# The keys' first weight pieces: split in front of block 2's transposes, or one at a time behind block 3's

## The chip, the core and the metric

The kernel runs on one core of a Trainium2 chip. The core's engines take their instructions each from a queue of its own and wait for one another through semaphores: TensorE (PE in the profile, with its weight loads listed as PEld) does matrix products and transposes into PSUM; VectorE (DVE) and ScalarE (ACT) work element by element and read PSUM; GpSimd (POOL) does some elementwise work; SyncE (SP) issues nearly all DMA transfers. The metric is the device time of one execution in microseconds (us), lower is better.

## The reference

A two-layer decoder over 512 positions of width 1024. The first layer has a dilated windowed attention, the second a "forgetting" attention on keys and values that are projected once from the residual stream behind the first layer. Each layer ends in a gated feed-forward block with a short causal convolution. Cut to the place of the change:

```python
kvf  = rms_norm(h, kv_norm) @ w_kvf          # h is the residual stream after layer 0
k_sh = kvf[..., :B_WIDTH]                    # keys, 16 heads of 64
v_sh = kvf[..., B_WIDTH:2 * B_WIDTH]         # values
log_f = log_sigmoid(kvf[..., 2 * B_WIDTH:] + b_f)
c_sh = cumsum(log_f, axis=1)                 # bias of the forgetting attention
mix  = fox_mixer(rms_norm(h, g[0]), w_q_b, w_o_b, k_sh, v_sh, c_sh)
```

## The kernel before, in words

The 512 positions are four blocks (0 to 3) of 128. Every large product is made from three: both operands are split into a rounded high part and the low rest, and `mm3` (L229 to L231) adds high x high, high x low and low x high.

**Weights.** All weights come in pieces of 128 x 1024 numbers, in one fixed list. The class `Weights` carries each piece through three steps: `load` issues its DMA on SP into a raw buffer (L41), `high` casts it on ACT (L49) and `low` subtracts on DVE (L55); the pair is then ready for TensorE. `split(n)` runs the last two steps for all pieces below number n, and calls `load` for two pieces more. `get()` hands out the next pair and first splits as far as `ahead` tells: `self.split(self.n_get + self.ahead - 1)`, where `n_get` counts the pieces handed out. There are nine raw buffers (shared with other tiles of that size), and a load waits until its buffer is free.

**Order.** The program is written out by hand: each engine runs its instructions in the order in which the Python code issues them. Nothing is reordered by a scheduler. Buffers are taken from pools, and the semaphores that make a tile's user wait for its last readers come from that.

**Behind the first feed-forward block.** Its down-projection finishes the residual stream h block by block. For each block the class `SharedBoundary` has two steps. `norm(b)` takes the statistics on ACT and scales the block on DVE (xn, L413). `transpose(b)` transposes it on TensorE in eight pieces (L424, into two PSUM banks xt_ps); DVE multiplies by a gain (xf, L426); ACT rounds that to the high part (xkh, L431), DVE subtracts the low part (xkl, L432), and ACT keeps an ungained copy for the queries (nT, L434). xkh, xkl and nT come in two halves of 512 features each.

**First half of the values.** Blocks 0 and 1 are transposed while the down-projection still runs. Then block 3 is normed, and the values' first 512 columns are computed. Four weight pieces (512 x 512 by two of the eight feature groups each) are used over six steps: blocks 0 and 1 with pieces 0 and 1, then blocks 0 and 1 with pieces 2 and 3, then block 2 with 0 and 1, block 2 with 2 and 3, and the same for block 3. Block 2 is transposed in the middle of the second step, block 3 behind the third. The sums lie in four PSUM banks (v_ps), from which DVE (blocks 0 and 2) and ACT (blocks 1 and 3) copy them to Vt (L908).

**Behind it.** The keys follow in eight groups of 128 columns (k_ps, `keys(c)`), each with one weight piece; then the gates' bias (f_ps, behind the second key group), the second half of the values, the queries and the attention (scores s_ps).

When the first value product is reached, pieces 0 to 3 of this part (the values' weights) are already split. `ahead` is 4 there. So the second, third and fourth `get` each split one more piece, which is the weight of the key groups 0, 1 and 2.

Of the kernel before, what the change touches and what calls it, by code (L numbers as in the profile page):

```python
# [70 lines left out]
def trunk_kernel(ctx, tc, x, norm_gains, w_qkv_a, w_o_a, w_q_b, w_o_b, kv_norm, w_kvf, b_f,  # L71
# [11 lines left out]
    def t8(shape, dt=F32, name="t8"):  # L83
        return p8.tile(shape, dt, tag="t8", name=name)
# [7 lines left out]
    def bank(shape, name="bank"):  # L92
        return psp.tile(shape, F32, tag="ps", name=name)
# [68 lines left out]
    W = Weights(nc, new_raw, lambda: t8([128, 2, 1024], F32R, name="w"), pieces)  # L162
# [732 lines left out]
    def values(banks, w, s, blocks):  # L895
        for b in blocks:
            for k in range(2):
                kc = 2 * s + k
                ah, al = xs(bd2.xT, kc, slice(b * 128, b * 128 + 128))
                mm3(banks[b], ah, al, w[0][:, k, :], w[1][:, k, :], kc == 0, kc == KD - 1)  # L900

    def value_weight():
        return [t.rearrange("p (k c) -> p k c", k=2) for t in W.get()]

    def keep_values(hf, b, o):
        if b == 0:
            Vt[hf] = t8([128, 4, 512], name=f"Vt{hf}")
        (act.copy if b % 2 else dve.tensor_copy)(Vt[hf][:, b, :], o)  # L908

    bd2.norm(3)  # L910
    banks = [bank([128, 512], name="v_ps") for _ in range(4)]
    wv = []
    for sp_, blocks in ((0, (0, 1)), (2, (0, 1)), (0, (2,)), (2, (2,)), (0, (3,)), (2, (3,))):
        if len(wv) < 4:
            wv += [value_weight(), value_weight()]
        for b in blocks:
            for s in (sp_, sp_ + 1):
                values(banks, wv[s], s, (b,))
            if (sp_, b) == (2, 0):
                bd2.transpose(2)  # L920
                W.ahead = 3
        if (sp_, blocks) == (0, (2,)):
            bd2.transpose(3)
        if sp_ == 2 and blocks[-1] > 1:
            for bb in (blocks[0] - 2, blocks[0]):
                keep_values(0, bb, banks[bb])
# [305 lines left out]
```

## Time and profile before

| | |
|---|---|
| median of 3 runs | 1169.48 us (1168.93 to 1169.65) |
| profiled execution | 1168.88 us, its span 1167.1 us |
| TensorE busy | 1153.6 us of the span |
| VectorE, ScalarE, GpSimd busy | 663.8, 515.8, 203.9 us |
| DMA | 115.72 MB, 99 GB/s on average |

Times in the profile's lists are microseconds from the start of the span. A timeline row has the start, the length, the engine, the line of the source, the operation, "result <- inputs", and the number of instructions merged into the row; in brackets, where it is given, stands how long the engine had been idle before the row and who ended that wait. Lengths of neighbouring TensorE rows overlap, since products are pipelined: what a product costs is the distance to the next start. The chain of waits goes back from the last instruction and names at each step what released it.

### The profile page before, as it was taken

To read this page: it belongs to the slowest core of one execution; us is meant where nothing else is said; L and a number is where in the kernel's file an instruction comes from. 1 tells how busy PE (TensorE), PEld (TensorE's weight loads), DVE (VectorE), ACT (ScalarE), POOL (GpSimd) and SP (SyncE) were. 2 spreads that over 40 slices of the span, in tenths; PEclk is the share of its full clock that TensorE was granted. 3 is DMA by queue.
4 is the path that set the end of the run, shared out by engine and by line. 5 is a ranking of instruction groups with operands and counts; after the bars stand their busy time and mean duration, and the time that the engine had idled before them with its cause. 6 is when DMAs were issued, how large, how long until landed. Compare 5 with 4: busy or idle time off the path is not lost.

```text
span 1167.1 us, 15131 instructions
## 1 busy us (share of the span) xinstructions
PE 1153.6 (99%) x5898; PEld 960.1 (82%) x5898; DVE 663.8 (57%) x991; ACT 515.8 (44%) x900; POOL 203.9 (17%) x231
## 2 busy tenths in 40 slices
PE   9999999999999999999999999999999999999997
PEld 6888889888888888888778888789888888888886
DVE  6433586655655674406464788757566566575304
ACT  5444665333433463306462677755433334354202
POOL 2722000212212210000000565400122122120000
PEclk9999999999999999999999999999999999999999
DMA  8131063333333355203204344264332332244001
GB/s 294 53 110 37 3 182 109 103 97 108 90 91 108 93 167 169 60 1 85 81 1 128 100 119 126 76 201 126 91 109 83 99 108 88 93 145 162 1 1 72
DMA packets 134849, 115.72 MB, mean 99 GB/s; under 512 B 5753, under 2 KB 119913, under 8 KB 134778
## 3 DMA queue, kind: packets, MB, share of 16 engines
q1 hardware_dynamic: 133498, 110.57, 31.0%
q0 software_dynamic: 1280, 4.20, 1.5%
q8 instruction: 46, 0.75, 0.3%
q14 instruction: 25, 0.20, 0.1%
HBM read 108.41 MB, written 2.15 MB: 95 GB/s over the span
## 4 chain that ended last, share of the span: by engine, by line
PE 89%; DVE 5%; ACT 3%; issue 2%; DVEq 0%; ACTq 0%
PE up L231 12%; PE up L229 12%; PE up L230 12%; PE acc L229 9%; PE acc L230 9%; PE acc L231 9%; PE v_ps L229 2%; PE v_ps L231 2%; PE v_ps L230 2%; PE qk_ps L230 2%; PE qk_ps L229 2%; PE qk_ps L231 2%; PE first L229 1%; PE first L230 1%; PE first L231 1%
## 5 line engine op out<-in xcount | busy, mean ns | idle before, releaser
L55 DVE TENSOR_TENSOR w<-wraw,w 128x1024 fp32r<-128x1024 f32 x182 | 262.3, 1467 | 93.5 <-ACT w L49 93.0
L49 ACT CAST w<-wraw 128x1024 fp32r<-128x1024 f32 x182 | 184.9, 1048 | 61.6 <-PE acc L231 38.3
L517 ACT ACTIVATE bb<-up,conv 128x512 f32<-128x512 f32 x80 | 62.4, 780 | 272.8 <-PE up L231 272.8
L525 POOL TENSOR_TENSOR hT<-bb 128x512 f32<-128x512 f32 x44 | 92.8, 2108 | 490.8 <-DVE bb L520 348.9
L518 DVE SCALAR_TENSOR_TENSOR bb<-up,conv,bb 128x511 f32<-128x511 f32 x80 | 60.0, 749 | 173.0 <-ACT bb L517 173.0
L229 PE MATMUL acc<-w,hs 128*128 128x512 f32 (+1 forms) x356 | 138.0, 388 | 1.1 <-DVE mix L276 1.1
L230 PE MATMUL acc<-w,hs 128*128 128x512 f32 (+1 forms) x356 | 137.8, 387 | 0.0
L231 PE MATMUL acc<-w,hs 128*128 128x512 f32 (+1 forms) x356 | 137.8, 387 | 0.0
L229 PE MATMUL up<-xbh,w 128*128 128x512 f32 x320 | 124.6, 389 | 0.0
L230 PE MATMUL up<-xcl,w 128*128 128x512 f32 x320 | 124.6, 389 | 0.0
L231 PE MATMUL up<-xbh,w 128*128 128x512 f32 x320 | 124.6, 389 | 0.0
L230 PE MATMUL up<-xbl,w 128*128 128x512 f32 x320 | 124.6, 389 | 0.0
L229 PE MATMUL up<-xch,w 128*128 128x512 f32 x320 | 124.6, 389 | 0.0
L231 PE MATMUL up<-xch,w 128*128 128x512 f32 x320 | 124.6, 389 | 0.0
L229 PEld LDWEIGHTS acc<-w,hs 128*128 128x128 f32 x356 | 66.9, 188 | 14.9 <-DVE mix L276 1.3
L231 PEld LDWEIGHTS acc<-w,hs 128*128 128x128 f32 x356 | 66.9, 188 | 13.5
L230 PEld LDWEIGHTS acc<-w,hs 128*128 128x128 f32 x356 | 66.9, 188 | 13.5
L231 PEld LDWEIGHTS up<-xch,w 128*128 128x128 f32 x320 | 60.1, 188 | 12.6
L229 PEld LDWEIGHTS up<-xbh,w 128*128 128x128 f32 x320 | 60.1, 188 | 12.5
L230 PEld LDWEIGHTS up<-xbl,w 128*128 128x128 f32 x320 | 60.1, 188 | 12.5
L230 PEld LDWEIGHTS up<-xcl,w 128*128 128x128 f32 x320 | 60.1, 188 | 12.5
L231 PEld LDWEIGHTS up<-xbh,w 128*128 128x128 f32 x320 | 60.1, 188 | 12.3
(241 smaller groups left out, 2085.7 us busy)
## 6 DMA issues: line engine op xcount, KB each, us to landing
wraw<-in_w_up_dram SPq DMA_DIRECT2D x88, 512.0 KB
wraw<-in_w_down_dram SPq DMA_DIRECT2D x44, 512.0 KB
wraw<-in_w_kvf_dram SPq DMA_DIRECT2D x16, 512.0 KB
wraw<-in_w_qkv_a_dram SPq DMA_DIRECT2D x16, 256.0 KB
wraw<-in_w_q_b_dram SPq DMA_DIRECT2D x8, 512.0 KB
ck<-cd SPq DMA_DIRECT2D x8, 512.0 KB
qst<-qst POOLq DMA_DIRECT2D x16, 256.0 KB, 3.5
wraw<-in_w_o_b_dram SPq DMA_DIRECT2D x8, 512.0 KB
```

What stands on the lines that cost most here:

```text
L49: self.nc.scalar.copy(pair[:, 0], raw)
L55: self.nc.vector.tensor_tensor(pair[:, 1], raw, pair[:, 0].bitcast(F32), ALU.subtract)
L229: pe.matmul(o, ah, bh, start=first, stop=False, skip_group_check=shared)
L230: pe.matmul(o, ah, bl, start=False, stop=False, skip_group_check=shared)
L231: pe.matmul(o, al, bh, start=False, stop=last, skip_group_check=shared)
L517: act.activation(bb[:, s, :], ps, AF.Identity, bias=cp[:, 3, ch:ch + 1], scale=cp[:, 2, ch:ch + 1])
L518: dve.scalar_tensor_tensor(bb[:, s, 1:], ps[:, :T - 1], cp[:, 1, ch:ch + 1], bb[:, s, 1:], ALU.mult, ALU.add)
L525: pool.tensor_tensor(hT[c // 4][:, c % 4, :], bb[:, 0, :], bb[:, 1, :], ALU.mult)
```

## The change

`ahead` is set to 1 in front of the first value product, so that the four `get` calls split nothing. It is set to 3 behind block 3's transposes; before, it was set to 3 behind block 2's. From the third step on, one piece is split behind each step, as long as no more than three are ahead of the last one handed out. This gives three splits: one behind block 3's transposes, one behind the second step of block 2, and one behind the first step of block 3. The second stands in front of the copies of the finished values of blocks 0 and 2, the third behind them. The same three pieces are split as before, the products are the same and stand in the same order.

```diff
     bd2.norm(3)
     banks = [bank([128, 512], name="v_ps") for _ in range(4)]
     wv = []
+    W.ahead = 1
     for sp_, blocks in ((0, (0, 1)), (2, (0, 1)), (0, (2,)), (2, (2,)), (0, (3,)), (2, (3,))):
         if len(wv) < 4:
             wv += [value_weight(), value_weight()]
@@
                 values(banks, wv[s], s, (b,))
             if (sp_, b) == (2, 0):
                 bd2.transpose(2)
-                W.ahead = 3
         if (sp_, blocks) == (0, (2,)):
             bd2.transpose(3)
+            W.ahead = 3
+        if blocks[0] > 1:
+            W.split(min(W.n_split + 1, W.n_get + W.ahead))
         if sp_ == 2 and blocks[-1] > 1:
             for bb in (blocks[0] - 2, blocks[0]):
                 keep_values(0, bb, banks[bb])
```

## The prediction

> **What bounds the kernel now.** I read the page first, then the list of what TensorE waited for, then the chain of waits, and last the timelines of the engines around the edited lines.
>
> ```profile
> span 1167.1 us, 15131 instructions
> PE 1153.6 (99%) x5898; PEld 960.1 (82%) x5898; DVE 663.8 (57%) x991; ACT 515.8 (44%) x900; POOL 203.9 (17%) x231
> PEclk9999999999999999999999999999999999999999
> ```
>
> TensorE (PE) is busy 99% of the span, at a granted clock of nine tenths or more in every slice. So almost all that an edit of orders on ACT (ScalarE) and DVE (VectorE) can change is one of TensorE's few waits. The longest but one is the only one in the edited stretch with a length that matters (who waited, for whom, us in total, times, longest):
>
> ```profile
> PE v_ps L229 <- ACT xkh L431: 1.4, 1, 1.4
> ```
>
> A product of the values (v_ps) waited once, 1.4 us, for the high halves of the transposed input (xkh). The chain of waits says what made them late (start, length, engine, result, line):
>
> ```profile
> 552.77 0.95 ACT w L49
> 553.81 0.90 issue
> 554.89 2.35 DVE w L55 x2
> 557.24 0.61 DVE xf L426
> 557.88 0.63 ACT xkh L431
> 558.55 0.50 PE v_ps L229
> ...
> 652.00 0.49 PE s_ps L1072 x4
> ```
>
> The weight splits (cast on L49, subtraction on L55) stand in front of block 2's scaling (xf), its rounding (xkh) and so the product. After that every link is TensorE until 652.00, where the attention begins with its first scores, again a TensorE instruction.
>
> **Part 1: the three splits leave the place in front of block 2.** TensorE's rows at that place, and DVE's and ACT's:
>
> ```profile
> 553.35 1.03 PE L424 MATMUL xt_ps<-ident,xn 128*128 128x128 f32 x8
> ...
> 556.74 0.39 PE L231 MATMUL v_ps<-w,xkl 128*128 128x512 f32 x1
> 558.55 0.50 PE L229 MATMUL v_ps<-w,xkh 128*128 128x512 f32 x1 [1.42 <-ACT xkh L431]
> 558.89 0.39 PE L230 MATMUL v_ps<-w,xkh 128*128 128x512 f32 x1
> 559.27 0.50 PE L231 MATMUL v_ps<-w,xkl 128*128 128x512 f32 x1
> 559.61 0.39 PE L229 MATMUL v_ps<-w,xkh 128*128 128x512 f32 x1
> ...
> 561.68 1.03 PE L424 MATMUL xt_ps<-ident,xn 128*128 128x128 f32 x8
> ...
> 570.73 0.39 PE L229 MATMUL k_ps<-xkh,w 128*128 128x512 f32 x1
> ...
> 576.17 0.39 PE L229 MATMUL k_ps<-xkh,w 128*128 128x512 f32 x1
> ```
>
> ```profile
> 553.00 0.75 DVE L413 TENSOR_SCALAR xn<-h,rs 128x1024 f32<-128x1024 f32 x1
> 553.75 3.50 DVE L55 TENSOR_TENSOR w<-wraw,w 128x1024 fp32r<-128x1024 f32 x3
> 557.16 1.28 DVE L426 TENSOR_TENSOR xf<-xt_ps,gcol 128x512 f32<-128x512 f32 x2
> 558.53 1.29 DVE L432 TENSOR_TENSOR xkl<-xf,xkh 128x512 fp32r<-128x512 f32 x2
> 562.32 1.29 DVE L426 TENSOR_TENSOR xf<-xt_ps,gcol 128x512 f32<-128x512 f32 x2 [2.49 <-PE xt_ps L424]
> 563.70 1.29 DVE L432 TENSOR_TENSOR xkl<-xf,xkh 128x512 fp32r<-128x512 f32 x2
> 564.91 1.28 DVE L908 COPY Vt<-v_ps 128x512 f32<-128x512 f32 x2
> ```
>
> ```profile
> 552.68 2.94 ACT L49 CAST w<-wraw 128x1024 fp32r<-128x1024 f32 x3
> ...
> 564.16 1.07 ACT L434 COPY nT<-xt_ps 128x512 f32<-128x512 f32 x2
> ```
>
> Block 2's transposes start at 553.35, but its xf starts only at 557.16, as the three subtractions end. Block 3 shows the step without splits: xf starts 562.32 - 561.68 = 0.64 after the transposes start. For block 2 that is 553.35 + 0.64 = 553.99, just after xn (553.00 + 0.75 = 553.75), which stays in front of it on DVE. So xf moves 557.16 - 553.99 = 3.17 earlier, and xkh and xkl, which follow it at once, do too. In the changed kernel's order of instructions nothing stands between xn and this xf on DVE, and ACT has block 2's xkh right behind the statistics of block 3.
>
> What TensorE then meets: undisturbed products start 0.227 apart (24 of a key take 576.17 - 570.73 = 5.44). The first product of block 2 is due at 556.74 + 0.23 = 556.97; its operand, which allowed the start at 558.55, now allows 558.55 - 3.17 = 555.38: spare 1.59. The first low half, used two products later (557.42), is there at 559.27 - 3.17 = 556.10: spare 1.32. These spares are the cover; nothing else is late next. From the row at 556.74 to the one at 559.61 four steps took 2.87 in place of 4 x 0.227 = 0.91. **The gain is 2.87 - 0.91 = 1.96 us.** The list of waits counts 1.4 of it; the rest is the restart and the late low half.
>
> **Part 2: block 3, and the splits behind it.** Block 3's transposes come at 561.68 - 1.96 = 559.72. DVE is done with block 2 at 558.53 + 1.29 - 3.17 = 556.65, so block 3 keeps its pace. All that follows is due 1.96 earlier. The splits now queue behind block 3. ACT ends the copies nT at 564.16 - 1.96 + 1.07 = 563.27 and then casts three pieces (2.94) until 566.2. DVE starts a subtraction 553.75 - 552.68 = 1.07 after its cast, at 564.3, and takes 3.50 / 3 = 1.17 for each: 565.5, 566.7; then two value copies (1.28), 568.0; then the third, 569.2. What DVE has to do next for the keys is this:
>
> ```profile
> 577.58 1.39 DVE L890 TENSOR_TENSOR kst<-k_ps,kst 64x512 fp32r<-64x512 f32 x2 [11.39 <-ACT kst L887]
> ```
>
> Key 0 starts at 570.73 - 1.96 = 568.77 and uses its low half two products later, at 569.22: spare 569.22 - 565.5 = 3.7. Key 1 starts at 576.17 - 1.96 = 574.21, over 7 behind its weight, and key 2 behind key 1, when its own has long been split. What is queued behind the moved work has room as well: the next on DVE, which stood idle 11.39 before the first key's kst subtraction, is due at 577.58 - 1.96 = 575.62; on ACT it is the value copies, and in the changed order the first later product that takes a bank of these values is one of key 3. So the splits cost nothing where they go; what is gone is lead: key 0's low half was done at 553.75 + 1.17 = 554.9 for a use at 570.73 + 0.45 = 571.2, 16.3 ahead, and is now 3.7 ahead.
>
> **Part 3: loads and waits.** The same loads stand in the same order on SP; POOL's list is unchanged. But the buffers of the raw pieces come free later:
>
> ```profile
> 556.13 0.37 SPq L41 DMA_DIRECT2D wraw<-in_w_q_b_dram  x1
> 615.98 1.05 ACT L49 CAST w<-wraw 128x1024 fp32r<-128x1024 f32 x1
> ```
>
> In the order before, the load of the query piece (556.13) waits for the second key's subtraction (553.75 + 2 x 1.17 = 556.09); in the changed order it waits for the first key's, which ends at 565.5. The load ahead of it waits for block 3's transposes, the one behind it for the second subtraction. Nothing in that queue is wanted soon: this piece is cast at 615.98 - 1.96 = 614.0, 48 us on. Zero.
>
> In the changed order the first product of each of keys 0 to 2 waits for ACT as well as for PE's own earlier writes, and a later one for DVE; two waits take an extra semaphore instruction, two more of them on PE. What such a one lasts:
>
> ```profile
> L229 PEldq EVENT_SEMAPHORE  x4: 51/51/51, 543.8 to 621.9; - x4
> ```
>
> Bounds: zero if it runs ahead of the array, 2 x 0.051 = 0.10 if both are exposed. I take zero, since what they wait for is done 3.7 and more before the product is due. The Trainium skill, page "Perfetto Trace Analysis", section "Identifying Dependency Chains", says that waits on several engines can be put into separate semaphore instructions ahead of the instruction; it speaks against the change, and with its price exposed the sum would be 1.86 in place of 1.96.
>
> **The sum.** The profiled execution took 1168.88 for its span of 1167.1; less 1.96 that is 1166.92. The median of the runs, 1169.48, lies 0.60 above it, so the forecast is 1169.48 - 1.96 = **1167.5 us**, 0.17% faster. A measurement of this kernel tells about 0.2%, or 2.34 us, from no change: the forecast lies just inside that.
>
> **Rivals.**
> *The gain measures above 2.34.* The runs before spread over 0.72 (1168.93 to 1169.65); half of it, 0.36, on top of 1.96 is 2.32. The low halves' and the high halves' waits may also be longer in executions without the profiler, which run 0.60 longer. Time: 1166.5 to 1167.1. For it: the wait is plainly removed and I have counted only its profiled size. Against: no second wait in the chain goes.
> *The gain is given back.* Some later stage is set by something that does not move. The candidate is the attention from 652.00. Against: its first link is a TensorE instruction and its loads, copies and gates all follow TensorE's products. Time: 1168.5 to 1169.5.
> *The key weights come too late, and it is slower.* Place: key 0's low half, which has 3.7 left of 16.3. ACT and DVE take their queues in order, so whatever holds ACT behind block 3 (a late nT copy, a late raw piece) holds cast, subtraction and key. It costs nothing up to 3.7, eats the gain at 3.7 + 1.96 = 5.7, and is slower by over 0.2% from 8.0. At 9 us it would give 1169.48 - 1.96 + 5.3 = 1172.8. For it: the lead shrinks to a quarter. Against: the longest single piece of work in that queue is about 1.3, and all three raw pieces had landed by 552.68 + 2 x 0.98 = 554.6, when the third cast ran; their loads wait for the same instructions in the changed order.
> *The change does not do what it says.* If block 2's xf still started after 555.3 (557.16 - 555.3 = 1.9 earlier only), part of the wait would stay, down to 1169.5. The order on DVE speaks against it.
>
> **How the numbers follow.** Forecast (gain of 1.2 to 2.34): 0.60. Above 2.34: 0.27. Given back, or half done: 0.07, within 0.2%. Key weights late: 0.06. So faster by over 0.2% 0.27, within 0.2% 0.67, slower 0.06. Range: at the low end 1.96 + 0.36 + 0.60 = 2.9, 1166.5; at the high end the 1.4 of the list less 0.10 and 0.36 would be 1168.5, and I reach on to 1169.1 to take in most of the given-back cases.
>
> **What the new profile would show.** Right: no PE wait on xkh in the value products, xf of block 2 within 0.3 of 554.0, key 0's products following block 3's last value product at 0.23, and all of TensorE's rows from the keys to the end 1.9 to 2.0 earlier. Wrong: a new PE or PEld wait of k_ps on w (L49 or L55), a wait of block 3's products on xkh or xkl, or a stage after 652 that is longer than before by the amount saved.

## The result and the profile after

| | before | changed |
|---|---|---|
| median of 22 runs each | 1169.24 us (1168.69 to 1170.19) | 1167.39 us (1166.55 to 1168.02) |
| ratio, 95% interval | | 0.9983 [0.9977, 0.9990] |
| span of the profiled execution | 1167.1 us | 1165.3 us |

The change gains 1.85 us, 0.16% (0.10 to 0.23%). The forecast was 1.96. The head of the new page, and all that TensorE waited for (who waited, for whom, us in total, times, longest):

```profile
span 1165.3 us, 15135 instructions
PE 1153.4 (99%) x5898; PEld 960.4 (82%) x5898; DVE 664.0 (57%) x991; ACT 516.0 (44%) x900; POOL 203.9 (17%) x231
```

```profile
PE o_ps L1123 <- ACT pT L1110: 1.5, 1, 1.5
PE warm L190 <- DVE zero L185: 1.4, 1, 1.4
PE acc L229 <- DVE mix L276: 1.1, 1, 1.1
PE qk_ps L230 <- DVE w L55: 0.8, 2, 0.6
PE pT_ps L1108 <- DVE nm L1084: 0.4, 1, 0.4
PE xt_ps L424 <- DVE xn L413: 0.4, 1, 0.4
PE pT_ps L636 <- DVE st L599: 0.2, 1, 0.2
```

The busy times of all engines are those of before: the work is the same. The entry of v_ps for xkh is gone from the list, and none of k_ps for a weight has come. The chain of waits now runs on TensorE from the transposes of block 1 to the attention's first scores, with no split, scaling or rounding in it:

```profile
541.65 1.09 PE xt_ps L424 x8
553.66 0.87 PE xt_ps L424 x8
560.00 0.88 PE xt_ps L424 x8
618.29 0.35 PE cq_ps L1026 x4
618.63 0.43 PE v_ps L229
650.15 0.49 PE s_ps L1075 x4
```

TensorE, DVE and SP at the place of the change:

```profile
553.50 1.04 PE L424 MATMUL xt_ps<-ident,xn 128*128 128x128 f32 x8
...
556.89 0.39 PE L231 MATMUL v_ps<-w,xkl 128*128 128x512 f32 x1
557.12 0.39 PE L229 MATMUL v_ps<-w,xkh 128*128 128x512 f32 x1
557.35 0.39 PE L230 MATMUL v_ps<-w,xkh 128*128 128x512 f32 x1
557.57 0.39 PE L231 MATMUL v_ps<-w,xkl 128*128 128x512 f32 x1
557.80 0.39 PE L229 MATMUL v_ps<-w,xkh 128*128 128x512 f32 x1
...
559.84 1.03 PE L424 MATMUL xt_ps<-ident,xn 128*128 128x128 f32 x8
...
568.66 0.39 PE L231 MATMUL v_ps<-w,xkl 128*128 128x512 f32 x1
568.89 0.39 PE L229 MATMUL k_ps<-xkh,w 128*128 128x512 f32 x1
```

```profile
554.13 1.29 DVE L426 TENSOR_TENSOR xf<-xt_ps,gcol 128x512 f32<-128x512 f32 x2 [0.23 <-PE xt_ps L424]
555.51 1.29 DVE L432 TENSOR_TENSOR xkl<-xf,xkh 128x512 fp32r<-128x512 f32 x2
560.48 1.29 DVE L426 TENSOR_TENSOR xf<-xt_ps,gcol 128x512 f32<-128x512 f32 x2 [3.67 <-PE xt_ps L424]
561.86 1.29 DVE L432 TENSOR_TENSOR xkl<-xf,xkh 128x512 fp32r<-128x512 f32 x2
564.38 2.36 DVE L55 TENSOR_TENSOR w<-wraw,w 128x1024 fp32r<-128x1024 f32 x2 [1.22 <-ACT w L49]
566.65 1.28 DVE L908 COPY Vt<-v_ps 128x512 f32<-128x512 f32 x2
567.85 1.22 DVE L55 TENSOR_TENSOR w<-wraw,w 128x1024 fp32r<-128x1024 f32 x1
```

```profile
565.63 0.37 SPq L41 DMA_DIRECT2D wraw<-in_w_q_b_dram  x1
```

The four products from 556.89 to 557.80 take 0.91 us; before, the same four took 2.87. Block 2's xf now waits 0.23 us for its transposes in place of three subtractions. Nothing of that is given back: block 3's transposes stand at 559.84 (561.68 before), the first key at 568.89 (570.73), the first scores at 650.15 (652.00), and the span ends 1.8 earlier.

### The profile page after: what moved, and what is told of

It is laid out like the page before. It is cut to its first block, busy times and chain, and to the rows that moved or that the text cites. A ratio compares the mean times of both kernels' runs of the same rounds, so it can differ in the third digit from the quotient of the medians.

```text
span 1165.3 us, 15135 instructions
## 1 busy us (share of the span) xinstructions
PE 1153.4 (99%) x5898; PEld 960.4 (82%) x5898; DVE 664.0 (57%) x991; ACT 516.0 (44%) x900; POOL 203.9 (17%) x231
## 4 chain that ended last, share of the span: by engine, by line
PE 91%; DVE 4%; ACT 3%; issue 2%; DVEq 0%; ACTq 0%
PE up L229 12%; PE up L231 12%; PE up L230 12%; PE acc L229 9%; PE acc L231 9%; PE acc L230 9%; PE v_ps L229 2%; PE v_ps L231 2%; PE v_ps L230 2%; PE qk_ps L230 2%; PE qk_ps L229 2%; PE qk_ps L231 2%; PE first L231 1%; PE first L229 1%; PE first L230 1%
## 5 line engine op out<-in xcount | busy, mean ns | idle before, releaser
L229 PE MATMUL acc<-w,hs 128*128 128x512 f32 (+1 forms) x356 | 137.9, 387 | 1.1 <-DVE mix L276 1.1
L229 PE MATMUL up<-xbh,w 128*128 128x512 f32 x320 | 124.5, 389 | 0.0
L229 PE MATMUL up<-xch,w 128*128 128x512 f32 x320 | 124.5, 389 | 0.0
L229 PEld LDWEIGHTS acc<-w,hs 128*128 128x128 f32 x356 | 66.8, 188 | 14.8 <-DVE mix L276 1.3
L229 PEld LDWEIGHTS up<-xbh,w 128*128 128x128 f32 x320 | 60.1, 188 | 12.4
```

Source lines behind the costliest of these rows:

```text
L229: pe.matmul(o, ah, bh, start=first, stop=False, skip_group_check=shared)
```

## The experiments

Two theories stood against each other at first. The cover theory is that of the prediction: only the DVE time ahead of block 2's xf counts, its first 1.3 us are free, and the rest goes to the end in full. The per-split theory says that each of the three splits cost a third of the gain, wherever it comes from. Then each side of a split, another place behind block 2, and the rival of late key weights were tried by themselves. All kernels start from the changed one unless it is said otherwise; medians are of 11 runs, with the ratio to the kernel before on the same chip and its 95% interval. The intervals are as wide as many of the differences that matter here, so a reading rests on the rows of the profiles as well.

**one_front, two_front, four_front: how many splits stand in front.** The one edit is the number that was 1:

```diff
-    W.ahead = 1
+    W.ahead = 2      # one_front;  3: two_front;  5: four_front
```

> One of the three splits goes back in front of block 2's transposes; the other two stay behind block 3's. Cover theory (only the time that DVE spends ahead of block 2's xf counts, and the first 1.3 us of it are free): one subtraction of 1.17 us puts off xf by 0.9 us, less than the 1.3 us spare, so no wait on xkh or xkl and the time of the changed kernel, 1167.4 us. Per-split theory (each split ahead of block 2 costs a third of the gain): 1167.4 + 0.6 = 1168.0 us.

> Two of the three splits in front of block 2's transposes, one behind block 3's. Cover theory: xf is 2.1 us later than in the changed kernel, 0.8 us over the 1.3 us spare; with the restart 0.8 to 0.9 us are lost: 1168.3 us, and the profile shows a wait of a value product on xkh or xkl of about half the old one. Per-split theory: 1167.4 + 1.2 = 1168.6 us. If one_front is free and this one is not, the cover is what decides.

> Four splits in front of block 2's transposes (one more than before the change; it is the one that stood behind the first key group). Cover theory: the wait of before grows by one whole subtraction, 1.17 us: 1169.24 + 1.2 = 1170.4 us. Per-split theory: 1169.24 + 0.6 = 1169.9 us. A theory in which the gain came from block 3 or from the keys expects 1169.2 us.

Measured: 1167.13 us (0.9983 [0.9974, 0.9991]), 1168.01 us (0.9990 [0.9981, 0.9999]) and 1171.59 us (1.0018 [1.0009, 1.0028]). One split in front is free, and its profile has no wait at that place. Two are not: on the same chip the slowest run of one_front (1167.45) is faster than the fastest of two_front (1167.52). The timeline of two_front shows a part of the old wait:

```profile
556.56 0.39 PE L231 MATMUL v_ps<-w,xkl 128*128 128x512 f32 x1
557.23 0.50 PE L229 MATMUL v_ps<-w,xkh 128*128 128x512 f32 x1 [0.28 <-ACT xkh L431]
...
557.95 0.50 PE L231 MATMUL v_ps<-w,xkl 128*128 128x512 f32 x1
558.29 0.39 PE L229 MATMUL v_ps<-w,xkh 128*128 128x512 f32 x1
```

The counted wait of 0.28 is less than the expected half of the old one. With the late low half and the restart (the time beyond the counted wait until products follow at 0.23 again) the four steps take 1.73 us in place of 0.91, and that loss of 0.82 is the expected one.

So the cost is not shared among the splits: it starts where the cover ends. The third point missed by 1.2 us; the list of waits of four_front has the wait at the expected 2.6, so the missing time is not in the wait. It is taken up below (gap_filled).

**dummy_front: the DVE time by itself.**

```diff
             if (sp_, b) == (2, 0):
+                scratch = W.new_pair()
+                for _ in range(3):
+                    dve.tensor_tensor(scratch[:, 1], h[:, 0, :], h[:, 1, :], ALU.subtract)
                 bd2.transpose(2)
```

> The changed kernel with three extra subtractions of 128 x 1024 numbers on DVE in front of block 2's transposes; they read two blocks of the residual stream and write a scratch tile that nobody reads. The splits themselves stay behind block 3's transposes, and so do their casts, loads and buffers. Cover theory: the DVE time alone brings the old wait back: 1169.2 us, with the value product's wait on xkh at 1.4 us. Theory that the casts on ACT, or the later loads and buffers, were what mattered: 1167.4 us.

Measured: 1169.29 us (1.0001 [0.9993, 1.0010]), the kernel before again, though its splits, casts, loads and buffers are where the changed kernel has them. The wait is back in its list:

```profile
PE v_ps L229 <- ACT xkh L431: 1.6, 1, 1.6
```

It is a little longer than the old 1.4, as the three extra subtractions take 3.74 us in place of 3.50.

**casts_front: the ACT side by itself.** The three casts are issued in front of `bd2.transpose(2)`, and the three subtractions stay at the three places of the changed kernel.

```diff
             if (sp_, b) == (2, 0):
+                cast = []
+                for n in range(W.n_split, W.n_split + 3):
+                    W.load(n + 3)
+                    raw, pair = W.raw.pop(n), W.new_pair()
+                    act.copy(pair[:, 0], raw)
+                    cast.append((raw, pair))
                 bd2.transpose(2)
@@
-            W.split(min(W.n_split + 1, W.n_get + W.ahead))
+            if cast:
+                W.half_done.append(cast.pop(0))
+                W.low()
```

> Only the casts on ACT go back in front of block 2's transposes, all three; the three subtractions on DVE stay where the changed kernel has them. Cover theory: ACT is held until about 555.8 us, block 2's xkh starts 0.9 to 1.0 us later than in the changed kernel, within the spare of 1.3 us: 1167.4 us and no wait. Theory that the casts carried half of the old wait: about 1168.3 us.

Measured: 1167.10 us (0.9983 [0.9975, 0.9992]): the casts in front cost nothing. They do reach into block 2's step, as DVE's timeline of this kernel shows, but within the cover:

```profile
553.78 1.29 DVE L426 TENSOR_TENSOR xf<-xt_ps,gcol 128x512 f32<-128x512 f32 x2 [0.21 <-PE xt_ps L424]
555.98 1.29 DVE L432 TENSOR_TENSOR xkl<-xf,xkh 128x512 fp32r<-128x512 f32 x2 [0.90 <-ACT xkh L431]
```

**behind_two: another place behind.** All three splits come right behind block 2's transposes:

```diff
                 bd2.transpose(2)
+                W.split(W.n_get + 3)
```

> All three splits right behind block 2's transposes, in front of block 3's. Cover theory: block 2 is as free as in the changed kernel; the three subtractions end at about 561.6 us and put off block 3's xf by 1.0 to 1.1 us, within block 3's spare of 1.2 us: 1167.4 us, no wait or one of 0.1 us. If the place behind block 3, or the spreading one by one, is part of the gain: up to 0.6 us more, 1168.0 us, with a wait of block 3's value products.

Measured: 1167.16 us (0.9983 [0.9974, 0.9992]), and no wait of a value product. The subtractions end at 561.58, as expected, and put off block 3's xf to 561.49 (1.6 behind the start of its transposes in place of 0.64); that lies in block 3's cover:

```profile
558.08 3.50 DVE L55 TENSOR_TENSOR w<-wraw,w 128x1024 fp32r<-128x1024 f32 x3 [1.22 <-ACT w L49]
561.49 1.28 DVE L426 TENSOR_TENSOR xf<-xt_ps,gcol 128x512 f32<-128x512 f32 x2
```

So neither the place behind block 3 nor the splitting one at a time is part of the gain; it is enough that the splits stand behind block 2's transposes.

**too_late: the rival put where it must bite.**

```diff
-        if blocks[0] > 1:
-            W.split(min(W.n_split + 1, W.n_get + W.ahead))
@@
+    W.split(W.n_get + W.ahead)
     del wv
```

> All three splits behind the last value copies, that is as late as the program allows before the first key. The rival of the prediction (key weights too late) put where it must bite. Cover theory: the first cast stands on ACT behind the copy of block 3's values (569.1 us) and ends near 570.7 us, its subtraction near 571.9 us; key 0's first product is due at 568.9 us and its low half at 569.35 us, so TensorE waits 1.8 us and then 0.7 us more: 1167.4 + 2.6 = 1170.0 us, with waits of k_ps on w. If the lead of the key weights didn't matter: 1167.4 us.

Measured: 1171.06 us (1.0015 [1.0006, 1.0024]), slower than before. The two waits are those that were worked out: key 0's first product starts 1.78 later than it would at the usual distance of 0.23, and its third 0.69 later. The list counts 1.62 and 0.53 of them:

```profile
570.78 0.50 PE L229 MATMUL k_ps<-xkh,w 128*128 128x512 f32 x1 [1.62 <-ACT w L49]
571.12 0.40 PE L230 MATMUL k_ps<-xkl,w 128*128 128x512 f32 x1
572.04 0.50 PE L231 MATMUL k_ps<-xkh,w 128*128 128x512 f32 x1 [0.53 <-DVE w L55]
```

The profiled execution took 1170.39, near the expected 1170.0. But the runs reach from 1169.87 to 1172.02, and the median missed by 1.1.

**gap_filled, too_late_filled, before_filled: what a long wait costs beside its length.** The misses of four_front and too_late have nearly the same size. Four_front's windows show why (stretch, length, busy time and count of PE, PEld, DVE, ACT and POOL, then TensorE's granted clock, DMA share and GB/s):

```profile
557.40:560.00 2.60, 0.04 (x1) 0.00 (x0) 2.51 (x5) 0.66 (x2) 0.00 (x0) 0.93 1.05 342
560.00:562.00 2.00, 1.99 (x5) 1.56 (x6) 1.28 (x2) 1.53 (x3) 0.00 (x0) 0.50 1.12 327
562.00:564.00 2.00, 2.00 (x8) 1.63 (x7) 0.00 (x0) 0.00 (x0) 0.00 (x0) 0.74 0.43 155
```

The granted clock falls to 0.50 at about 559.6, still within the wait of 2.6 us, and stays there until about 563.0, some 3.4 us. TensorE starts 5 products in 2 us there, where it starts 8 or 9 at full clock. To test this, eight products whose result nobody reads were put into the wait; in too_late seven stand in front of key 0, and in the kernel before five stand in its old wait.

```diff
+        if (sp_, blocks) == (2, (0, 1)):          # gap_filled, on four_front
+            spare = bank([128, 512], name="spare")
+            for _ in range(8):
+                pe.matmul(spare, xs(bd2.xT, 0, slice(0, 128))[0], wv[0][0][:, 0, :], start=True, stop=True)
         if (sp_, blocks) == (0, (2,)):
             bd2.transpose(3)
```

> The kernel with four splits in front of block 2 (four_front), and eight products of block 0 into a spare bank that nobody reads, placed where TensorE waits for block 2. Four_front took 1171.6 us in place of the 1170.4 expected, and its profile shows a granted clock of 0.50 for 3.4 us right behind the wait of 2.6 us. Clock theory (the long idle time brought the clock down, and that is the missing 1.1 us): the eight products shorten the idle time to about 0.8 us, the clock stays at 1.00 there, the operands come no earlier, and the time is 1170.4 us. Theory that the fourth split costs more for another reason (its load, its buffer, the keys' order): still 1171.6 us.

> The kernel too_late, with seven products into a spare bank that nobody reads in front of key 0, where TensorE waits for the key's weight. Too_late took 1171.1 us in place of 1170.0; its profiled execution (1170.39) had full clock at that place, but its runs reach from 1169.9 to 1172.0. Clock theory (in some executions the two waits there bring the granted clock down, and in others not): with 1.6 us of the idle time filled the upper runs go, and the median is about 1170.2 us. Theory that the wait on the key weights is simply longer than I worked out: 1171.1 us as before.

> The kernel before the change, with five products into a spare bank in the place of the old 1.4 us wait; they are 1.1 us long and the operands come no earlier. If the old wait cost only its own length, as the prediction has it: 1169.2 us, no difference. If in some executions it also brought the clock down (the 22 runs of before lie about two values, 1169.0 and 1169.55): about 1169.0 us and a smaller spread.

Measured: gap_filled 1170.41 us (1.0009 [1.0000, 1.0018]), that is 1.2 us faster than four_front (which ran on another chip) with eight more products to do, and the value that was expected of four_front. Block 2's first operand comes no earlier (560.02, four_front 560.01), but the clock stays up:

```profile
557.40:560.00 2.60, 1.88 (x9) 1.22 (x7) 2.52 (x4) 0.65 (x2) 0.00 (x0) 1.00 1.04 332
560.00:562.00 2.00, 1.98 (x7) 1.35 (x8) 1.29 (x2) 1.55 (x3) 0.00 (x0) 1.00 1.11 331
562.00:564.00 2.00, 2.00 (x15) 1.72 (x13) 0.20 (x1) 0.00 (x0) 0.00 (x0) 1.00 0.42 153
```

Too_late_filled took 1169.88 us (1.0005 [0.9996, 1.0014]), 0.3 below the expected 1170.2, and its runs end at 1170.64: the upper ones are gone. That fits the clock, but the profile of too_late had full clock at key 0, so there the cause is inferred from the two sets of runs and not seen. Before_filled took 1169.19 us (1.0000 [0.9991, 1.0008]): the old wait of 1.4 us cost its length and, in the median, no clock. Its runs spread less than those of the kernel before on that chip (1168.80 to 1169.66 against 1168.68 to 1170.58), but 11 runs against 21 do not settle that.

**norm_first: the next wait in front.** The list of TensorE's waits has one more entry in this stretch, 0.4 us for xn at block 1's transposes. Block 1 is normed ahead of block 0's transposition, for that one step:

```diff
+        def half(self, b, hf, o):                 # in SharedBoundary
+            if (b, hf) != (2, 0):
+                return super().half(b, hf, o)
+            self.mix.half(b, hf, o)
+            self.norm(1)
+            self.transpose(0)
```

> The changed kernel, and at the first half of the last down-projection block but one, block 1 is normed before block 0 is transposed (the two steps trade places for that block alone). TensorE still waits 0.4 us for block 1's xn at its transposes near 541.6 us, because ACT rounds and copies block 0 first. Cover theory: xn of block 1 comes 2 us earlier, the wait and its restart go, 0.6 us: 1166.8 us, faster than both kernels. If block 0's xkh and xkl then come too late for the first value products at 545.3 us, a wait appears there and the gain is lost: 1167.4 us or more.

Measured: 1166.42 us (0.9976 [0.9967, 0.9984]), the fastest of all here, 0.7 us below casts_front and behind_two, which ran on the same chip and equal the changed kernel. The expected gain was 0.6, and the rows account for 0.64: from the last product in front of block 1's transposes to the first value product it is 544.78 - 540.93 = 3.85 us, in the changed kernel 545.33 - 540.84 = 4.49. The transposes follow the products in front of them at once, where the changed kernel's stood at 541.65 behind a last product at 540.84:

```profile
540.93 0.40 PE L231 MATMUL acc<-w,hs 128*128 128x512 f32 x1
541.16 1.03 PE L431 MATMUL xt_ps<-ident,xn 128*128 128x128 f32 x8
```

## Why the prediction was right, step by step

**Part 1, the wait that goes.** Forecast: xf of block 2 at 553.99, no wait, 1.96 us. In the new trace xf starts 554.13 - 553.50 = 0.63 behind the start of the transposes (0.64 forecast), the four products take the forecast 0.91, and the gain at the place is 2.87 - 0.91 = 1.96. What TensorE's later rows show is 1.84, since this execution was already 0.15 later when it reached the place (553.50 for 553.35). The last part of the text asked for 1.9 to 2.0 there; that bound was too narrow for two single executions. The spares of 1.59 and 1.32 us are bracketed: in one_front xf starts 0.9 later behind its transposes than in the changed kernel, and that is free; in two_front it is 2.04 later and 0.82 is lost, so about 1.2 were covered; a delay of 0.8 through ACT is free (casts_front). That it was the subtractions and not the casts, loads or buffers rests on dummy_front and casts_front.

**Part 2, the splits behind block 3.** Forecast: first subtraction at 564.3, value copies at 566.7, the third done at 569.2. Measured: 564.38, 566.65 and 567.85 + 1.22 = 569.07. Key 0 follows the last value product by 0.23 without a wait. Too_late shows that lead is what pays for this.

**Part 3, loads and waits.** The query piece's load was forecast for 565.5 and stands at 565.63; nobody waits for it. The two extra semaphore instructions are there: between 540 and 640 us TensorE's queue has six at L229 in place of four, 51 ns each. No delay from them is seen: key 0 follows at 0.23. Of the two sums, 1.96 and 1.86, the medians' 1.85 cannot choose; the rows at key 0 speak for zero. The section "Identifying Dependency Chains" of the Trainium skill's page "Perfetto Trace Analysis" is right that such instructions are there, but here they cost nothing.

**The sum.** The median of three runs on which the forecast stood, 1169.48, was 0.24 above that of the 22 runs. Together with a gain 0.11 too large this partly cancels, so it is in part luck that 1167.5 lies so near to 1167.39; the gain is the number to judge by.

**The rivals.** More than 2.34 did not come: I had no mechanism for it beyond the spread of the runs. The 0.60 by which the median lay above the profiled execution need not come from longer waits: the last section shows that executions differ by about 0.5 in the attention. Nothing was given back: the first scores moved by 1.85. Late key weights did not happen, but too_late makes it a real case. The price was right in the profiled execution; what the working lacked is that a long wait can cost clock as well.

## What to carry to other kernels

Where a busy engine waits, ask which queue the late operand passed through and what stood in front of it there: work that is wanted 16 us later had been queued ahead of work that was wanted at once. Such an edit is worth the length of the wait with its restart (here 1.96 us, of which the list counted 1.4), as long as the wait is too short to cost clock; count the cover on both sides, since up to its edge a delay is free and beyond it every part of a microsecond goes to the end. Moved work has an edge of its own at the other end (here some 4 us), so the middle of the slack is the place for it.

## What the runs showed of the hardware that I had not expected

A wait of TensorE of 2.6 us cost 1.1 us more than its length: the granted clock fell to 0.50 for about 3.4 us, from 0.4 us before the wait ended, and the 12 products up to block 3's transposes took 564.27 - 560.01 = 4.26 us in place of 563.17 - 560.02 = 3.15 with the gap filled. Two of the 11 runs of four_front, at 1170.15 and 1170.17, were as fast as with the gap filled; the others lay at 1171.4 to 1171.9. Waits of 1.4 us (before) and 1.6 us (dummy_front, too_late) were followed by full clock in their profiles. The Trainium skill, page "TensorE: Matmul & The Clock Gate", section "Part 1: The HAM clock gate (the "warmup" mystery)", says that TensorE falls to half its clock after at least one idle window of about 3.4 us, and that these windows run free of the kernel. The half rate agrees with four_front's rows; the wait that set it off, 2.57 us, was shorter than such a window, and here the measurement decides. Why some executions escape was not tried.

In four profiled executions (dummy_front, casts_front, too_late, gap_filled) the clock falls as well in the attention, where TensorE has gaps of its own; too_late's, for one:

```profile
738.00:741.00 3.00, 3.00 (x12) 2.33 (x11) 2.93 (x8) 1.73 (x7) 1.03 (x3) 0.58 0.49 128
```

The kernels before and after the change had full clock there in their profiles. From the first scores to the end of the span these four executions take 515.6 to 515.8 us, and the nine others 515.1 to 515.2, so an execution with the fall is about 0.5 us longer there. That is also the distance between the two values about which the 22 runs of the kernel before lie, 1169.0 and 1169.55; that these come from it was not shown run by run.
